# A hybrid diffusion step on one core: block 1's x loaded behind w_ada, its lora-downs moved into the recurrence list, lora-up shared out between ScalarE and GpSimd

## The chip, the core and the metric

The kernel runs on one NeuronCore of a Trainium2 chip. Its engines work side by side: TensorE (PE in the profile; PEld is its weight load), VectorE (DVE), ScalarE (ACT), GpSimd (POOL) and SyncE (SP), whose queue issues most of the transfers. Each engine runs its own instructions in the order in which they stand, and waits on semaphores where it needs another engine or a transfer. The metric is the device time of one execution in microseconds; lower is better.

## What is computed

One layer for 2176 tokens, 128 of context and 2048 of an image, each with 1024 channels. In the reference, cut to what matters here:

```python
mod = silu(c) @ w_ada + b_ada                    # shift, scale, gate of 1024 each, per kind of token
h   = rmsnorm(x, norm_g) * (1 + scale) + shift
r, k, v, g_a, b_gate, c_gate, u_conv, g_b = split(h @ w_in)     # 8 parts of 512 channels
r, k, v = token_shift(r, k, v)                   # q + mu * (0.5 * (prev + next) - q)
# _wkv, for both directions e:
lw = tanh(h @ decay_down[e])                     # 1024 -> 64     "lora-down"
w  = decay_w0[e] + lw @ decay_up[e]              # 64 -> 512      "lora-up"
la = h @ iclr_down[e]
a  = sigmoid(iclr_bias[e] + la @ iclr_up[e])
decay = exp(-exp(-softplus(-w) - 0.5))
kk = k * kk_scale, normalised per head
# then a delta-rule scan over the tokens in both directions, group norm, a gate
# group B: y = b_gate * conv3(c_gate * u_conv) * silu(g_b)
# both groups @ w_out, gate, residual; at the end one more rmsnorm
```

## The kernel before

All of it is in float32. A product on TensorE is made of three: each operand is split into a high part, rounded to the format TensorE reads, and a low part, the rest; high times high, high times low and low times high are summed. ScalarE usually makes the high part (a copy), VectorE or GpSimd the low part (a subtraction). A weight tile of `w_in` (128 rows of output, 512 KB) comes in by `raw_w` (L145), gets its high part by `high_w` (L150) and its low part by `low_w` (L154), and both parts are written back (L155), so that later thirds load them ready-made.

The program has three phases; the change lies in the opening of the first. Phase 1 goes over the tokens in blocks of 384 (`BLK`), two blocks to a third. For each third it forms the normalised `h` of both blocks, the lora-downs, then `recurrence`: eight units, four groups of 128 channels times two blocks. A unit makes the products of v, k, g and r (`mmv`, `mmk`, `mmg`, `mmr`), the lora-ups (`upa` for the learning rate, `upw` for the decay, L452), the sums per head (`psss` from kk, `psbb`), and writes the operands of the scan to HBM (`scr_ops` from the tile `xs`, L330). Then comes group B, with `mmb`, `mmc`, `mmu`, `mmgb`; inside it x of the next third is loaded and normalised (`x2`, `x3`), and the gate rows of `w_ada` come in (`wgate`).

Order: outside the recurrence a scheduler orders the instructions of each engine at build time. In the recurrence two lists of words, `UNIT_FIRST` and `UNIT`, give the order by hand for PE, DVE, ACT and POOL.

The opening before: `w_ada` comes in four slices of two pieces, 1 MB each (L265); PE forms the modulation rows from them (`psrow`, L212), VectorE copies these (`modrow`), PE turns them (`psmod`), and VectorE forms gs and sh, one pair for each half of the channels. Block 0's x (`x0`) is squared, summed by PE (`psq`), rooted on ScalarE (`rt`, L241), inverted on VectorE (L243). `make_h` then runs per 128 channels: L170 on VectorE (x times gs times rt), L171 on ScalarE (plus sh: the high part), L172 on VectorE (the low part). `first_products` forms block 0's products with the lora weights w32, w33 and with the k and r weights w4, w0 (all `mmf`) in two halves of the channels, as the halves of h appear. `lora_down` takes such a product through Tanh or Copy on ScalarE into `lf` (L664), and VectorE makes a high and a low part of each direction, `lw` (a cast, L668, a subtraction, L669). For block 1 it forms the products itself (`mml`, 48 of them). `load_up` loads the lora-up weights (`upraw`, 1 MB) and splits them into `ups` on VectorE (L125, L126).

Buffers: the pool `hl` holds two large tiles of tag "h", first the `w_ada` slices `wadas1` and `wadas2`, later h and others; tag "x" of `ta_` holds one tile, x0, then `upraw`, then `xs`, then x2; tag "upx" of `ca` holds x1, then `ups`. A new tile waits until the readers of the one before it in its buffer are done.

## Time and profile before

| | |
|---|---|
| median of 3 runs | 1640.9 us (1639.54 to 1645.43) |
| profiled execution | 1643.1 us, span 1641.3 us |
| mean granted TensorE clock | 0.967 |
| busy, share of the span | PE 92%, DVE 70%, ACT 47%, POOL 34% |
| chain that ended last | PE 66%, DVE 15%, DMA 8%, issue 5%, ACT 3% |
| the stretch of the change | 0 to 90.5 us (the opening and unit 0's products) |
| recurrence of the first third | 90.5 to 240 us, PE 144.92 us busy |
| its group B | 240 to 392 us |

A row of the timeline gives the start, the time from the first start to the last end of a run of like instructions, engine, line, operation, output and inputs, shapes, the count, and in brackets how long the engine had stood idle before and what ended that. A row of the windows gives a stretch, its length, the busy time of PE, PEld, DVE, ACT and POOL with the number of instructions, the granted clock, the share of the DMA engines and GB/s. A row of the waits gives who waited for whom, the sum, how often, and the longest. Line numbers are those of the kernel before; behind the change, lines past 256 are one to seven higher.

### The profile page before, as it was taken

The numbers are of one execution on the slowest core, as the hardware profiler recorded it, in microseconds if no ns is written. First come the engines' busy times: TensorE is split into PE (matmuls) and PEld (weight loads), VectorE is DVE, ScalarE is ACT, GpSimd is POOL, SyncE is SP. The second block draws the span as 40 slices with busy tenths as digits, with TensorE's granted clock in tenths as the row PEclk, the third lists the DMA queues.
The fourth block names the chain that finished last, engine by engine and source line by source line (L and its number), as shares of the span: only waits on it lengthen the run. The fifth ranks groups of instructions, "written<-read, shape, count | busy, mean of one in ns | idle before, by whom it ended". The sixth has DMA issues, their size and how long they took to land.

```text
span 1641.3 us, 41749 instructions
## 1 busy us (share of the span) xinstructions
PE 1518.0 (92%) x17364; PEld 1401.0 (85%) x17364; DVE 1141.3 (70%) x1960; ACT 773.5 (47%) x1494; POOL 560.8 (34%) x961
## 2 busy tenths in 40 slices
PE   5899989999999999999999989999898897599998
PEld 2899988889999999999999988888787786478786
DVE  5899993744699945459974456898888987446433
ACT  4466652511555413136531137778677776322222
POOL 0034330000233200013314507788778766112221
PEclk7799999999999999999999999999999998899999
DMA  9559998654578864438986635656566654455442
GB/s 372 199 148 263 271 258 291 239 193 162 153 209 216 225 224 165 163 115 253 243 240 231 229 104 156 176 154 184 155 183 179 162 144 151 118 170 173 136 147 96
DMA packets 204589, 313.94 MB, mean 191 GB/s; under 512 B 58088, under 2 KB 147560, under 8 KB 190320
## 3 DMA queue, kind: packets, MB, share of 16 engines
q1 hardware_dynamic: 168816, 311.13, 61.7%
q10 hardware_dynamic: 35584, 0.14, 1.5%
q8 instruction: 136, 2.23, 0.6%
q14 instruction: 53, 0.43, 0.1%
HBM read 208.05 MB, written 103.17 MB: 190 GB/s over the span
## 4 chain that ended last, share of the span: by engine, by line
PE 66%; DVE 15%; DMA 8%; issue 5%; ACT 3%; POOL 1%; SPq 1%; ACTq 0%; DVEq 0%; POOLq 0%
PE psE L1185 5%; PE psu L1500 4%; PE psS L1216 4%; PE psu L1501 3%; PE psu L1502 3%; PE psFm L1018 2%; PE psX L1167 2%; PE psGm L1018 2%; PE mmc L182 2%; PE mmb L184 2%; PE mmb L182 2%; PE mmb L183 2%; PE mmc L184 2%; PE mmc L183 2%; PE mmgb L182 1%
## 5 line engine op out<-in xcount | busy, mean ns | idle before, releaser
L1090 POOL TENSOR_TENSOR zt<-zt,ztmp 128x30 f32<-128x30 f32 (+7 forms) x510 | 206.8, 405 | 39.7
L1087 POOL TENSOR_TENSOR ztmp<-ab,zt 128x60 f32<-128x60 f32 (+7 forms) x255 | 136.5, 535 | 103.4 <-DVE ab L1078 79.7
L410 POOL TENSOR_TENSOR sh<-rawl 128x384 f32<-128x384 f32 (+1 forms) x48 | 48.0, 1017 | 252.1 <-ACT rawl L401 252.1
L1216 PE MATMUL psS<-sv,E 128*64 128x64 f32 x2176 | 101.8, 228 | 27.9 <-DVE so L1242 13.7
L1216 PEld LDWEIGHTS psS<-sv,E 128*64 128x64 f32 x2176 | 83.3, 138 | 46.1 <-issue 17.1
L1190 DVE TENSOR_TENSOR E<-psE,msk 128x512 f32<-128x512 f32 x136 | 90.9, 684 | 16.0 <-PE psE L1185 15.0
L1242 DVE TENSOR_TENSOR sv<-psS,pc 64x128 f32<-64x128 f32 x254 | 64.1, 275 | 43.5 <-PE psS L1216 42.6
L1565 POOL TENSOR_TENSOR z<-z,x 128x512 f32<-128x512 f32 x32 | 42.9, 1342 | 150.1 <-DVE z L1559 100.5
L1171 ACT ACTIVATE stf<-psX 64x512 f32<-64x512 f32 x136 | 80.5, 592 | 16.6 <-PE psX L1167 14.3
L434 POOL TENSOR_TENSOR hsl<-sq,hsh 128x384 fp32r<-128x384 f32 (+1 forms) x24 | 35.6, 1483 | 141.1 <-ACT hsh L429 141.1
L182 PE MATMUL mmg<-h,w 128*128 128x384 f32 (+1 forms) x216 | 70.8, 328 | 0.0
L183 PE MATMUL mmg<-h,w 128*128 128x384 f32 (+1 forms) x216 | 70.7, 327 | 0.0
L184 PE MATMUL mmg<-h,w 128*128 128x384 f32 (+1 forms) x216 | 70.6, 327 | 0.0
L182 PE MATMUL mmb<-h,w 128*128 128x384 f32 (+1 forms) x192 | 62.9, 328 | 5.7 <-DMA w<-scr_wsp 4.0
L182 PE MATMUL mmv<-h,w 128*128 128x384 f32 (+1 forms) x192 | 64.3, 335 | 2.8 <-ACT lf L664 2.2
L182 PE MATMUL mmc<-h,w 128*128 128x384 f32 (+1 forms) x192 | 64.1, 334 | 0.0
L184 PE MATMUL mmc<-h,w 128*128 128x384 f32 (+1 forms) x192 | 63.5, 331 | 0.6 <-DVE w L154 0.6
L184 PE MATMUL mmb<-h,w 128*128 128x384 f32 (+1 forms) x192 | 62.8, 327 | 1.2 <-DVE w L154 1.2
L183 PE MATMUL mmv<-h,w 128*128 128x384 f32 (+1 forms) x192 | 63.6, 331 | 0.0
L184 PE MATMUL mmv<-h,w 128*128 128x384 f32 (+1 forms) x192 | 63.5, 331 | 0.0
L183 PE MATMUL mmc<-h,w 128*128 128x384 f32 (+1 forms) x192 | 63.3, 330 | 0.0
L184 PE MATMUL mmu<-h,w 128*128 128x384 f32 (+1 forms) x192 | 62.6, 326 | 0.6 <-DVE w L154 0.6
(311 smaller groups left out, 5007.4 us busy)
## 6 DMA issues: line engine op xcount, KB each, us to landing
w<-scr_wsp SPq DMA_DIRECT2D x68, 1024.0 KB, 5.6
scr_wsp<-w SPq DMA_DIRECT2D x34, 1024.0 KB, 6.0
rr<-scr_ops SPq DMA_DIRECT2D x32, 1024.0 KB, 5.6
scr_ops<-xs SPq DMA_DIRECT2D x160, 192.0 KB, 6.2
wr<-in_win SPq DMA_DIRECT2D x34, 512.0 KB, 6.6
x<-in_x SPq DMA_DIRECT2D x17, 512.0 KB, 3.5
wadas<-in_wada SPq DMA_DIRECT2D x8, 1024.0 KB, 15.1
sv<-scr_vt SPq DMA_DIRECT2D x32, 256.0 KB, 3.8
```

The source lines that it names most:

```text
L182: T.matmul(ps[:, :n], w[:, 0, k], hh[:, 0, k, :n], start=k == 0, stop=False)
L183: T.matmul(ps[:, :n], w[:, 0, k], hh[:, 1, k, :n], start=False, stop=False)
L184: T.matmul(ps[:, :n], w[:, 1, k], hh[:, 0, k, :n], start=False, stop=k == 7)
L1018: T.matmul(dst(h, a, er), w[hr_, u, :], x(hr_, u), start=True, stop=True)
L1087: G.tensor_tensor(tv, ab[:, j:j + 2, j + 2:32].unsqueeze(1).broadcast_to((128, kn, 2, n)), zt[:, :kn, j:j + 2].unsqueeze(3).broadcast_to(( ...
L1090: G.tensor_tensor(zt[:, :kn, j + 2:32], zt[:, :kn, j + 2:32], tv[:, :, r], ALU.subtract)
L1171: P.activation(g.fs[64:128, :, hd, e::2], g.ps["X"][e][hr_].rearrange("p a (b t) -> p b a t", b=2), AF.Copy, scale=-1.0)
L1185: T.matmul(pe[r, i, hd, :].rearrange("p (b t) -> p b t", b=2), lt[:, b, hd, us.start + k + i], rt[:, :, hd, us.start + k + i], start=True, ...
L1190: V.tensor_tensor(g.E[n][:, k:k + 2].rearrange("p a b c -> p (a b) c"), pe[:].rearrange("p a b c -> p (a b) c"), B.msk[:, ME[g.d]].unsquee ...
L1216: T.matmul(g.sp[i // 4][r, q, hd, :], g.E[n][:, k, hd, r], g.sv[:, u, hd, :], start=True, stop=True)
L1242: V.tensor_tensor(dst, g.sp[i // 4][0:64, q], B.pc[0:64, d, 2 * p:2 * p + 2, c:c + 1].broadcast_to((64, 2, 64)), ALU.mult)
L1500: T.matmul(ps[:], mh[:, n], hi[:, cs], start=start and n == 0, stop=False)
```

## The change

Five things are done in the opening of phase 1.

1. x1 is loaded behind all of `w_ada`, between the weights w4 and w0, into the "h" buffer of `wadas1`, and no longer ahead of the last four pieces. w4 and w0 are asked for one step later in the program.
2. Block 1's norm stands behind all of block 0's first products. The lora's second half comes ahead of k and r, which run over all eight channel groups at a stretch.
3. Block 1's `lora_down` is called from the recurrence's list, at the first product on block 1, and so is the load of w12.
4. `load_up` casts on ScalarE and subtracts on GpSimd. The v weight w8 goes into the tile `wv` in tag "x", and its low part is made on GpSimd.
5. `lf` takes tag "bs" in place of "sq". In the first third `xs` takes an "h" buffer, so tag "x" is free for x2 once `wv` is read.

```diff
@@ -122,8 +122,8 @@
         parts = ca.tile([128, 8, 512], F32R, tag="upx", name="ups")
         hi, lo = [parts[:, i:i + 4].rearrange("p (n d) c -> p n d c", d=2) for i in (0, 4)]
         for n in range(2):
-            V.tensor_copy(hi[:, n], raw[:, n])
-            V.tensor_tensor(lo[:, n], raw[:, n], hi[:, n].bitcast(F32), ALU.subtract)
+            P.copy(hi[:, n], raw[:, n])
+            G.tensor_tensor(lo[:, n], raw[:, n], hi[:, n].bitcast(F32), ALU.subtract)
             for d in range(2):
                 up[n, d] = (hi[:, n, d], lo[:, n, d])
 
@@ -145,8 +145,8 @@
         nc.sync.dma_start(raw[:], A["win"][cb])
         return raw
 
-    def high_w(cb, raw):
-        w = wp.tile([128, 2, 8, 128], F32R, tag="w", name=f"w{cb}_{K.u()}", bufs=4)
+    def high_w(cb, raw, w=None):
+        w = w or wp.tile([128, 2, 8, 128], F32R, tag="w", name=f"w{cb}_{K.u()}", bufs=4)
         P.copy(w[:, 0], raw[:])
         return w
 
@@ -250,11 +250,11 @@
     hs = {}
     psf = []
 
-    def first_products(ws, ks):
+    def first_products(ws, ks, at=None):
         n = BLK[0][1]
         if ks[0] == 0:
             psf.extend(pmm.tile([128, 384], F32, tag="mm", name=f"mmf{i}_{K.u()}") for i in range(len(ws)))
-        for ps, w in zip(psf[-len(ws):], ws):
+        for ps, w in zip(psf[-len(ws):] if at is None else psf[at:], ws):
             products(ps, w, hs[0], n, ks)
 
     psm = {}
@@ -268,9 +268,10 @@
             x0 = load_x(0)
         if i == 1:
             wlora = [load_w(32), load_w(33)]
-            x1 = load_x(1, ca, "upx")
-        if i == 2:
-            ws0 = [load_w(cb) for cb in (4, 0)]
+        if i == 3:
+            ws0 = [load_w(4)]
+            x1 = load_x(1, hl, "h")
+            ws0.append(load_w(0))
         rows = tp.tile([128, 512], F32, tag="pv", name=f"modrow{b}", bufs=1)
         V.tensor_copy(rows[:], pr[:])
         hf = b % 2
@@ -292,11 +293,11 @@
         if i == 1:
             h0 = make_h(0, xb[0])
             next(h0)
-            xb[1] = norm(1, x1, V)
             first_products(wlora, range(4))
     next(h0)
-    first_products(ws0, range(4))
-    first_products(wlora + ws0, range(4, 8))
+    first_products(wlora, range(4, 8), 0)
+    first_products(ws0, range(8))
+    xb[1] = norm(1, x1, V)
 
 
     NRAW = 3
@@ -339,7 +340,7 @@
 
         one = lambda u, tag, pool=ta_, b=1, dt=F32: pool.tile([128, 384], dt, tag=tag, name=f"{tag}_{u.g}_{u.j}_{K.u()}", bufs=b)
         two = lambda u, tag: ta_.tile([128, 2, 384], F32, tag=tag, name=f"{tag}_{u.g}_{u.j}_{K.u()}", bufs=1)
-        xs = ta_.tile([128, 8, 384], F32, tag="x", name=f"xs{t3}")
+        xs = ta_.tile([128, 8, 384], F32, tag="x", name=f"xs{t3}") if t3 else hl.tile([128, 8, 384], F32, tag="h", name=f"xs{t3}")
         slot = dict(al=xs[:, 0:2], rh=xs[:, 2:4], ka=xs[:, 4:6], be=xs[:, 6:8])
         U = []
         for i, (g, j) in enumerate(units):
@@ -363,6 +364,9 @@
                 following[x] = dense(wts[x], hs[js[0]], BLK[js[0]][1], "cugb"["krvg".index(x)])
                 return
             u = U[i]
+            if u.j not in lws:
+                lws[u.j] = lora_down(u.j, *wlora, None)
+                wts["g"] = load_w(12)
             if x not in u.ps:
                 u.ps[x] = dense(wts[x], hs[u.j], u.n, x)
             if u.last:
@@ -660,7 +664,7 @@
         lw = [ta_.tile([128, 384], F32R, tag=f"lw{i}_{nm}", name=f"lw{i}_{j}") for i in range(4)]
         for which, (w, fn) in enumerate(((wd, AF.Tanh), (wi, AF.Copy))):
             ps = pre[which] if pre else dense(w, hs[j], n, f"l{which}")
-            f = ta_.tile([128, 384], F32, tag="sq", name=f"lf{which}_{j}", bufs=1)
+            f = ta_.tile([128, 384], F32, tag="bs", name=f"lf{which}_{j}", bufs=1)
             P.activation(f[:, :n], ps[:, :n], fn)
             for d in range(2):
                 a, b = slice(d * 64, d * 64 + 64), slice(64 - d * 64, 128 - d * 64)
@@ -675,14 +679,17 @@
         pre = {}
         for j in js:
             if j not in hs:
-                if t3 == 0:
-                    pre[0] = psf[2:]
-                    ws = ws0 + [load_w(cb) for cb in (8, 12)]
-                    nc.sync.dma_start(smask[:], A["cst"][:, 128:512])
                 run(make_h(j, xb[j]))
-            lws[j] = lora_down(j, wd, wi, psf[:2] if j == 0 else None)
-        if t3 == 0:
-            load_up()
+            if t3 or j == 0:
+                lws[j] = lora_down(j, wd, wi, psf[:2] if j == 0 else None)
+            if t3 == 0 and j == 0:
+                pre[0] = psf[2:]
+                nc.sync.dma_start(smask[:], A["cst"][:, 128:512])
+                load_up()
+                raw = raw_w(8)
+                wv = high_w(8, raw, ta_.tile([128, 2, 8, 128], F32R, tag="x", name="wv"))
+                low_w(8, raw, wv, G)
+                ws = ws0 + [wv, None]
         if t3:
             ws = [load_w(cb) for cb in (4, 0, 8, 12)]
         wts = dict(zip("krvg", ws))
```

On SP's queue, behind the last pieces of `w_ada` (`wadas`); `x_216` and `x_313` are x1, `wr_7` w4, `wr_9` w0, `wr_13` w8, `upraw` the lora-up weights, and `scr_wsp` the written-back parts. Before:

```order
L145 DMA wr_3_210<-in_win 128x1024 [waits DMAHW1_49]
L199 DMA x_216<-in_xt 128x8x384 [waits DMAHW2_49]
L265 DMA wadas_137<-in_wada 128x2048 [waits DMAHW3_49]
L265 DMA wadas_137<-in_wada 128x2048 [waits DMAHW4_49]
L265 DMA wadas_136<-in_wada 128x2048 [waits DMAHW5_49]
L265 DMA wadas_137<-in_wada 128x2048 [waits DMAHW6_49]
L681 DMA smask<-in_cst 128x384 [waits DMAHW7_49]
L155 DMA scr_wsp<-w_2_206 128x2048 [waits DMAHW0_49,DVE_49]
L145 DMA wr_7_326<-in_win 128x1024 [waits DMAHW1_49]
L155 DMA scr_wsp<-w_4_212 128x2048 [waits DMAHW2_49,DVE_49]
L145 DMA wr_9_332<-in_win 128x1024 [waits DMAHW3_49]
```

The same stretch in the changed kernel:

```order
L265 DMA wadas_137<-in_wada 128x2048 [waits DMAHW5_49]
L687 DMA smask<-in_cst 128x384 [waits DMAHW6_49]
L155 DMA scr_wsp<-w_2_206 128x2048 [waits DMAHW7_49,DVE_49]
L145 DMA wr_7_307<-in_win 128x1024 [waits DMAHW0_49]
L155 DMA scr_wsp<-w_4_212 128x2048 [waits DMAHW1_49,DVE_49]
L145 DMA wr_9_315<-in_win 128x1024 [waits DMAHW2_49]
L199 DMA x_313<-in_xt 128x8x384 [waits DMAHW4_49,DMAHW3_49,PE_49]
L155 DMA scr_wsp<-w_8_309 128x2048 [waits DVE_49]
L145 DMA wr_13_505<-in_win 128x1024 [waits DMAHW5_49,DMAHW0_49]
```

x1 has moved from ahead of four `w_ada` pieces to behind w0, and waits for PE, which must have read `wadas1`. Further on the same queue, in unit 0's spills, x2 (`x_2815`) now stands:

```order
L331 DMA scr_ops_59<-xs_536 128x384 [waits DMAHW4_49]
L199 DMA x_2815<-in_xt 128x8x384 [waits DMAHW5_49,PE_49]
L155 DMA scr_wsp<-w_55_820 128x2048 [waits DMAHW6_49,DVE_49]
```

Before, it stood behind the whole recurrence, in group B.

On VectorE, from the end of block 0's h; `rt_284` and `rt_460` are block 1's inverse roots, `lw_0` the lora-down parts of block 0 and `lw_1` those of block 1, `h_509` and `h_511` block 1's h. Before:

```order
L243 RECIPROCAL rt_284<-rt_284 128x128 x3
L172 SCALAR_TENSOR_TENSOR h_229<-x_149,sh_363,h_229 128x256
L154 TENSOR_TENSOR w_10_334<-wr_9_332,w_10_334 128x1024
L170 SCALAR_TENSOR_TENSOR x_216<-x_216,gs_224,rt_284 128x384 x4
L170 SCALAR_TENSOR_TENSOR x_216<-x_216,gs_362,rt_284 128x384 x4
L172 SCALAR_TENSOR_TENSOR h_509<-x_216,sh_225,h_509 128x384 x4
L668 CAST lw_0_480<-lf_0_484 64x384
L668 CAST lw_0_481<-lf_0_484 64x384
L172 SCALAR_TENSOR_TENSOR h_509<-x_216,sh_363,h_509 128x384 x4
L417 TENSOR_TENSOR sh_0_21_617<-rawc_468 128x128
L669 TENSOR_TENSOR lw_0_480<-lf_0_484,lw_0_480 64x384
L669 TENSOR_TENSOR lw_0_481<-lf_0_484,lw_0_481 64x384
```

In the changed kernel, from the end of block 0's first lora-down:

```order
L243 RECIPROCAL rt_460<-rt_460 128x128 x3
L423 SCALAR_TENSOR_TENSOR ok_0_17_549<-sh_0_16_545,dv,q_0_0_14_540 128x384
L672 CAST lw_0_482<-lf_0_490 64x384
L672 CAST lw_0_483<-lf_0_490 64x384
L170 SCALAR_TENSOR_TENSOR x_313<-x_313,gs_222,rt_460 128x384 x4
L170 SCALAR_TENSOR_TENSOR x_313<-x_313,gs_327,rt_460 128x384 x4
L673 TENSOR_TENSOR lw_0_482<-lf_0_490,lw_0_482 64x384
L673 TENSOR_TENSOR lw_0_483<-lf_0_490,lw_0_483 64x384
L172 SCALAR_TENSOR_TENSOR h_511<-x_313,sh_223,h_511 128x384 x4
L172 SCALAR_TENSOR_TENSOR h_511<-x_313,sh_328,h_511 128x384 x4
```

The reciprocal of block 1 and its eight L170 now stand behind block 0's first lora-down, and the eight stand ahead of the subtractions of the second.

On PE, from the end of the first products; `mml` are block 1's lora-downs. Before:

```order
L182 MATMUL mml_17_538<-h_509,w_2_206 128x384 [waits PE_49,Activation_49]
L182 MATMUL mml_18_569<-h_509,w_4_212 128x384 [waits Activation_49]
L183 MATMUL mml_17_538<-h_509,w_2_206 128x384 [waits DVE_49]
...
L184 MATMUL mml_18_569<-h_509,w_4_212 128x384
L452 MATMUL upa_20_614<-lw_0_482,ups 128x384 [waits DVE_49,Activation_49]
...
L182 MATMUL mmv_640<-h_229,w_14_498 128x384 [waits Activation_49]
...
L439 MATMUL psss_0_665<-hsh_0_25_627,onr 128x384 [waits Activation_49]
L440 MATMUL psss_0_665<-hsl_0_27_632,onr 128x384 [waits Pool_49]
```

The same place in the changed kernel:

```order
L227 MATMUL psq_457<-hslq_454,onf 128x384 [waits DVE_49]
L456 MATMUL upa_15_542<-lw_0_482,ups 128x384 [waits DVE_49,PE_49,Activation_49]
L456 MATMUL upa_15_542<-lw_0_482,ups 128x384 [waits Pool_49]
...
L182 MATMUL mmv_568<-h_227,wv 128x384 [waits Activation_49]
L183 MATMUL mmv_568<-h_227,wv 128x384
L184 MATMUL mmv_568<-h_227,wv 128x384 [waits Pool_49]
...
L443 MATMUL psss_0_593<-hsh_0_20_555,onr 128x384 [waits Activation_49]
L444 MATMUL psss_0_593<-hsl_0_22_560,onr 128x384 [waits Pool_49]
L182 MATMUL mml_27_603<-h_511,w_2_206 128x384 [waits Activation_49]
```

`mml` has moved from ahead of `upa` to behind `psss`, and the sum of squares `psq` of block 1 to the end of the first products; `upa` and `mmv` now also wait for GpSimd.

## The prediction

> **What bounds the kernel now.** I read the windows of the stretch that the change touches first, then the timelines of PE, DVE, ACT and POOL from 40 to 93 us, then the waits behind it. The first fence gives, per stretch, each engine's busy time, the granted clock and the share of the DMA engines.
>
> ```profile
> 35.00:40.00 5.00, 5.00 (x40) 3.28 (x36) 2.28 (x5) 1.04 (x2) 0.00 (x0) 1.00 1.03 423
> 40.00:45.00 5.00, 2.97 (x20) 1.77 (x12) 3.25 (x11) 2.81 (x6) 0.00 (x0) 0.77 0.60 248
> 69.80:90.50 20.70, 17.69 (x85) 16.84 (x85) 14.28 (x20) 9.99 (x20) 4.02 (x4) 0.84 0.42 153
> 90.50:240.00 149.50, 144.92 (x829) 141.52 (x827) 140.35 (x176) 92.70 (x165) 55.15 (x42) 1.00 0.96 252
> 300.00:340.00 40.00, 34.92 (x181) 30.07 (x180) 25.68 (x50) 12.86 (x20) 1.38 (x1) 0.96 0.66 233
> ```
>
> The DMA engines bound the first 41 us (share 1.03, 423 GB/s). From 90.5 us PE is busy 144.92 of 149.5 us: whatever makes it reach that point later is added to the end nearly one for one. So I ask when PE ends unit 0's last product (mmg), which it does at 90.4 now.
>
> ```profile
> 61.49 0.51 PE L182 MATMUL mml<-h,w 128*128 128x384 f32 x2
> 69.81 0.86 PE L452 MATMUL upa<-lw,ups 128*128 128x384 f32 x4
> 71.50 1.09 PE L452 MATMUL upw<-lw,ups 128*128 128x384 f32 x4 [0.83 <-ACT lf L664]
> 74.77 0.69 PE L182 MATMUL mmv<-h,w 128*128 128x384 f32 x1 [2.18 <-ACT lf L664]
> 81.91 0.34 PE L182 MATMUL mmk<-h,w 128*128 128x384 f32 x1
> 90.08 0.33 PE L184 MATMUL mmg<-h,w 128*128 128x384 f32 x1
> ```
>
> Between 61.49 and 69.81 PE forms block 1's 48 lora-down products (8.3 us) without a wait. They lie there under the VectorE work that upa needs:
>
> ```profile
> 48.86 2.57 DVE L243 RECIPROCAL rt<-rt 128x128 f32<-128x128 f32 x3
> 51.35 0.39 DVE L172 SCALAR_TENSOR_TENSOR h<-x,sh,h 128x256 fp32r<-128x256 f32 x1
> 52.79 4.33 DVE L170 SCALAR_TENSOR_TENSOR x<-x,gs,rt 128x384 f32<-128x384 f32 x8
> 59.14 0.74 DVE L668 CAST lw<-lf 64x384 fp32r<-64x384 f32 x2
> 62.71 1.14 DVE L669 TENSOR_TENSOR lw<-lf,lw 64x384 fp32r<-64x384 f32 x2
> 63.88 1.29 DVE L125 CAST ups<-upraw 128x1024 fp32r<-128x1024 f32 x2
> 65.09 0.61 DVE L419 SCALAR_TENSOR_TENSOR ok<-sh,dv,q 128x384 f32<-128x384 f32 x1
> 66.38 2.36 DVE L126 TENSOR_TENSOR ups<-upraw,ups 128x1024 fp32r<-128x1024 f32 x2
> 69.95 2.37 DVE L154 TENSOR_TENSOR w<-wr,w 128x1024 fp32r<-128x1024 f32 x2
> 82.11 0.56 DVE L442 TENSOR_SCALAR sq<-psss 128x384 f32<-128x384 f32 x1 [5.44 <-PE psss L440]
> ```
>
> Block 1's norm (the reciprocal at 48.86) is over before block 0's h is (51.35 + 0.39 = 51.74).
>
> **Part by part: x1 behind w_ada.** A load of x is 1536 KB, 1.57 MB; at 410 GB/s, a round figure under the 423 above, it takes 3.8 us.
>
> ```profile
> x<-in_xt SPq DMA_DIRECT2D x2, 1536.0 KB, 11.1
> 41.21 1.05 ACT L150 CAST w<-wr 128x1024 fp32r<-128x1024 f32 x1 [4.31 <-DMA wr<-in_win]
> 45.72 0.56 ACT L241 ACTIVATE rt<-psq,eps 128x384 f32<-128x384 f32 x1
> 56.53 1.28 ACT L664 ACT_TABLE_LOAD   x1 [0.89 <-PE mmf L184]
> 57.83 0.49 ACT L664 ACTIVATE lf<-mmf 128x384 f32<-128x384 f32 x1
> 60.50 0.58 ACT L405 ACTIVATE q<-mmf,dv 128x384 f32<-128x384 f32 x1
> ```
>
> With it out of the way, w4 lands at about 41.2 - 3.8 = 37.4, w0 at 41 and x1 itself at about 45. The end of block 0's h moves less than the loads, since the last w_ada products and gs still stand ahead of it and w4's low part (L154) no longer does: from 51.7 to about 50.5. That is the change's gain.
>
> **The norm behind the first products, and the price of it.** PE's products of lora on block 0 end 1 to 5 us after the last L172 (three late products, or 24 of the slow 0.32 us). With the table load and the Tanh (1.28 + 0.49) the first lf is done between 53.9 and 57.2; I take L = 56.4, near the upper end, since these products stand interleaved with k's and r's. From L the rows above lead to upa, which reads the lora-down parts of block 0: the cast of ssq and the copies of k (about 1.5, q alone 0.58), a table load back to Sqrt (1.28) and rt (0.56), L + 3.3; the reciprocal, 2.5, L + 5.8; ok and two casts, 1.3, L + 7.1; eight L170 of x1, 4.3, L + 11.4, which stand ahead of the last two subtractions of lora (1.1). So upa starts at L + 12.5 = 68.9, 0.9 earlier than its 69.81, but the 48 products of block 1 are now behind it. Before, PE needs 20.6 us from 69.81 to the end of mmg, of which 3.0 were waits for lf (0.83 + 2.18). After: 20.6 - 3.0 + 8.3 = 25.9, so mmg ends at 68.9 + 25.9 = 94.8: **+4.4 us**. By the bounds of L, upa starts between 66.4 and 69.7: +1.9 to +5.2. To break even it would have to start at 90.4 - 25.9 = 64.5.
>
> The two switches of table that are new beside this chain are priced by the 1.28 us row, and the next ACTIVATE starts 0.02 us behind it (57.83). The Trainium skill ("ScalarE: Activation LUTs", What ACT_TABLE_LOAD costs) gives 1283 ns for the load and another 1380 ns for a drain; this trace shows the first and not the second, and the one switch in the chain would cost 1.4 us more by the page.
>
> **Lora-up split off VectorE.** VectorE loses 1.29 + 2.36 of ups and 1.2 of w8. They don't come off the chain, which is the reciprocal, L170 and lora now. GpSimd gets three subtractions, and what these do to VectorE is the second price:
>
> ```profile
> 95.33 1.40 POOL L434 TENSOR_TENSOR hsl<-sq,hsh 128x384 fp32r<-128x384 f32 x1 [6.03 <-ACT hsh L429]
> 95.77 1.37 DVE L498 TENSOR_TENSOR bs<-kd 128x384 f32<-128x384 f32 x1
> 156.57 0.55 DVE L498 TENSOR_TENSOR bs<-kd 128x384 f32<-128x384 f32 x1
> 104.61 2.55 DVE L444 RECIPROCAL sq<-sq 128x384 f32<-128x384 f32 x1
> 105.25 2.41 POOL L154 TENSOR_TENSOR w<-wr,w 128x1024 fp32r<-128x1024 f32 x1 [1.95 <-ACT w L150]
> 114.49 1.22 DVE L154 TENSOR_TENSOR w<-wr,w 128x1024 fp32r<-128x1024 f32 x1
> ```
>
> L498 takes 0.55 us, but 1.37 when a GpSimd subtraction began 0.44 us ahead of it: it ends 0.41 us behind that. The reciprocal is not slowed (2.55) by a 2.41 us subtraction beneath it. So instructions with two operands from SBUF take turns with GpSimd. In the changed order ACT casts ups behind rt and the second lf, so GpSimd subtracts from about L + 4.9 to L + 9.7: the first half of that lies under the reciprocal up to L + 5.8, the rest (some 3.9) stands against ok and L170. The third, wv, starts about with the last L170 and stands against lora's subtractions (up to 2.4). Bounds 0 and +6.3; nearest the L498 row would be the upper end, but the last of them may fall between instructions: I take **+4.5 us**.
>
> The Trainium skill ("SBUF — State Buffer", SBUF: two separate sides) has GpSimd and VectorE share a port pair as "an exclusive lock, not a bandwidth split", held for a whole instruction, against VectorE's instructions with two SBUF inputs. The L498 and reciprocal rows agree with it, and by it alone the sum would hold 6.3 here.
>
> **Behind upa.** mmv needs wv's low part only now, at about 71; GpSimd is done with it then. Unit 0's chain on VectorE (L442 and the reciprocal) stood right behind psss, level with mmk (82.11 and 81.91). Now the casts and subtractions of block 1's second lora product (0.74 + 1.14) and w12's low part (1.2) stand between the last mml and it, so it starts some 3 us behind mmk. Does PE feel that? In the stretch behind, these were its longest waits:
>
> ```profile
> PE mmk L184 <- DVE w L154: 2.7, 3, 1.4
> ```
>
> VectorE is what PE waits for there, but it has 149.5 - 140.35 = 9.2 us of idle to catch up with: 0 to +3, I take **+1**.
>
> **x2 early.** Its load moves from group B, behind the recurrence, into unit 0's spills on SP's queue.
>
> ```profile
> 253.85 0.45 SPq L199 DMA_DIRECT2D x<-in_xt  x1
> 98.04 2.19 SPq L330 DMA_DIRECT2D scr_ops<-xs  x4
> 100.15 0.34 PE L184 MATMUL mmv<-h,w 128*128 128x384 f32 x1
> ACT ssq L234 <- DMA x<-in_xt: 4.9, 2, 3.2
> PE psgr L212 <- DMA wgate<-in_wada: 6.7, 1, 6.7
> ```
>
> SP issues those spills from 98.04 to 100.2. The load waits there for PE's mmv of the second unit, which ends at 100.5, so SP's queue, on which all spills and weights behind it stand, is held by little. But its 3.8 us of transfer enter a stretch whose DMA share is 0.96: 0 to +3.8, and I take **+0.5**, since a unit's weights are asked for one unit ahead. In group B, ACT no longer waits for x2 (part of 4.9 us), while the scheduler puts block 2's norm later there and block 3's too. The stretch 300 to 340 holds 5.1 us of PE idle, so -5.1 to +4: I take **-1**.
>
> Sum: 4.4 + 4.5 + 1 + 0.5 - 1 = **+9.4** on the profiled execution's 1643.1 us (span 1641.3): 1652.5. That execution is 2.2 above the median of the runs, 1640.9; against the median the forecast is **1650.3 us**. What a measurement here can tell from no change is about 0.5%, 8.2 us: below 1632.7 it is faster, above 1649.1 slower.
>
> **Rivals.** (1) *No turn-taking on the path*: GpSimd's subtractions fall under the reciprocal and into VectorE's waits for lf and rt, as the one at 105.25 does under a reciprocal. Against it stands the place: ups is cast only behind rt. Without the 4.5: 1645.8. (2) *The transfers bite*: x2's load pushes weights and spills of a saturated stretch by its 3.8 us in full, and the later norm in group B costs PE 1 us where I took a gain of 1. For it speaks the 0.96, against it that PE's longest waits there are for VectorE and none for a transfer. With 3.8 in place of 0.5, and +1 in place of -1, 1650.3 + 5.3 = 1655.6. (3) *Not slower*: with x2 in SBUF 150 us early, its norm never holds group B, and the 5.1 us of PE idle between 300 and 340 go whole. It decides once the opening loses under 5.1, that is with upa's start at the early bound and no turn-taking: 1640.9 + 1.9 - 5.1 = 1637.7. Against it: the longest PE wait there is for wgate (6.7), not for x2. (4) *The change doesn't do what it says*: x1's wait on PE's reading of w_ada (its buffer) might hold SP, behind which w8, w12 and ups stand. The last w_ada product is over before x1's bytes could flow (about 41), so I fold it into the first term.
>
> **How the numbers follow.** Forecast 0.44, own range 1647.5 to 1653.5; (1) 0.27; (2) 0.16; (3) 0.13. To hold 8 in 10 I cut the lower half of (1) and the most of (3), and let (2) stand in full: 1643 to 1657. Faster needs (3) at its far end, with the wgate wait gone too: 0.05. Slower: two thirds of the forecast's case (0.29) and (2), 0.45. No change: 0.50.
>
> **What would show it.** In the changed kernel's timeline: L172 of block 0 ends at about 50.5 (right: the load's gain is real); PE idle of some 10 us between psq and upa; upa's start at 68.9 plus the turn-taking, 73 (under 65 the forecast is wrong from the start); L170 or L673 rows of VectorE stretched to 1.5 us and more beside POOL's L126 rows (if they keep their 0.54 each, rival 1); mml behind psss, mmg's end at about 99 to 100; the window of 150 us behind it as busy as before (under 143 of 149.5: rival 2); PE idle of 5 us in the 40 us from about 309 (gone: rival 3).

## The result, and the profile after

The changed kernel takes 1654.0 us (median of 4 runs, 1652.1 to 1657.5) against 1640.2 for the kernel before; the ratio is 1.008, with a 95% interval of 1.0052 to 1.0109. A second comparison on another chip (the last run below, 12 executions) gave 1649.5 against 1639.8 and 1.006 (1.0037 to 1.0084). It is slower by 0.6 to 0.8%, 10 to 14 us; the forecast was 1650.3.

The profiled execution of the changed kernel took 1657.5 us (span 1655.7), 3.5 above its median. First PE around unit 0, in the timeline (lines from 257 on are numbered one to seven higher than before):

```profile
56.97 0.44 PE L227 MATMUL psq<-hslq,onf 128*128 128x384 f32 x1 [0.52 <-DVE hslq L219]
70.79 0.98 PE L456 MATMUL upa<-lw,ups 128*128 128x384 f32 x2 [13.38 <-DVE lw L673]
73.49 1.01 PE L456 MATMUL upa<-lw,ups 128*128 128x384 f32 x2 [1.72 <-DVE lw L673]
81.12 0.33 PE L182 MATMUL mml<-h,w 128*128 128x384 f32 x1
89.29 0.33 PE L184 MATMUL mml<-h,w 128*128 128x384 f32 x1
97.64 0.34 PE L184 MATMUL mmg<-h,w 128*128 128x384 f32 x1
```

PE stands idle for 13.38 us ahead of upa, where it formed block 1's lora-down products before, and forms them from 81.1 to 89.6 instead. The last product of unit 0 ends at 98.0; before it ended at 90.4. What PE waited for lay on VectorE, whose timeline shows the chain and what lay beside it on GpSimd and ScalarE:

```profile
49.83 0.74 DVE L172 SCALAR_TENSOR_TENSOR h<-x,sh,h 128x128 fp32r<-128x128 f32 x2
55.06 0.49 ACT L668 ACTIVATE lf<-mmf 128x384 f32<-128x384 f32 x1
58.79 2.58 DVE L243 RECIPROCAL rt<-rt 128x128 f32<-128x128 f32 x3
60.15 4.96 POOL L126 TENSOR_TENSOR ups<-upraw,ups 128x1024 fp32r<-128x1024 f32 x2 [2.76 <-ACT ups L125]
61.28 1.63 DVE L423 SCALAR_TENSOR_TENSOR ok<-sh,dv,q 128x384 f32<-128x384 f32 x1
62.84 2.88 DVE L672 CAST lw<-lf 64x384 fp32r<-64x384 f32 x2
65.75 4.32 DVE L170 SCALAR_TENSOR_TENSOR x<-x,gs,rt 128x384 f32<-128x384 f32 x8
70.10 3.34 DVE L673 TENSOR_TENSOR lw<-lf,lw 64x384 fp32r<-64x384 f32 x2
70.67 2.35 POOL L154 TENSOR_TENSOR wv<-wr,wv 128x1024 fp32r<-128x1024 f32 x1 [5.56 <-ACT wv L150]
```

Against the rows of the kernel before (0.61, 0.74 and 1.14 for ok, two casts and two subtractions), these took 1.0, 2.1 and 2.2 us longer, beside the GpSimd subtractions: 5.4 us together, 3.2 of them ahead of the first half of upa and 2.2 ahead of the second. The eight L170, between the two bursts, kept their 0.54 each.

Behind unit 0, the windows:

```profile
98.00:252.00 154.00, 145.94 (x829) 141.53 (x828) 146.03 (x180) 93.17 (x166) 52.74 (x42) 1.00 0.96 258
252.00:426.00 174.00, 163.54 (x888) 150.72 (x889) 89.84 (x176) 48.89 (x79) 7.05 (x6) 0.96 0.61 210
```

The recurrence needs 154.0 us for about the products that took 149.5 (829 matmuls in each); group B is shorter than before. The loss grew and shrank again, then. A table over all runs is made from the same marks of PE's timelines: the end of unit 0's last product, the start of psss in the second and the eighth unit and in the first unit of the second third, and the first product of phase 2 (psX, the end of phase 1). The first row is in us, all others are the difference to it. Each profile is one execution, all columns but the last two come from it; the ratios are against the kernel before on the same chip. The kernel before has one profile only, and most of the others were taken on other chips, where its median lay between 1639.8 and 1648.0 us.

| | unit 0's end | second unit | eighth unit | second third | end of phase 1 | ratio | 95% |
|---|---|---|---|---|---|---|---|
| before (us) | 90.4 | 100.3 | 220.4 | 422.6 | 986.7 | 1 | |
| changed | +7.6 | +8.0 | +12.0 | +7.9 | +8.0 | 1.008 | 1.0052 to 1.0109 |
| changed, again | +6.4 | +6.9 | +12.7 | +5.2 | +3.5 | 1.006 | 1.0037 to 1.0084 |
| a_low_v | +8.4 | +8.8 | +14.4 | +10.2 | +8.8 | 1.0065 | 1.0038 to 1.0091 |
| a_ups_v | +4.2 | +4.7 | +9.8 | +2.9 | +2.8 | 1.0024 | 1.0000 to 1.0049 |
| a_lora_ahead | +8.0 | +8.0 | +10.8 | +4.5 | +5.1 | 1.0061 | 1.0037 to 1.0085 |
| a_x1_early | +6.6 | +7.0 | +9.6 | +6.6 | +7.5 | 1.0068 | 1.0038 to 1.0097 |
| a_both_back | +2.3 | +2.2 | +5.4 | -2.0 | -3.6 | 1.0001 | 0.9975 to 1.0027 |
| a_x2_late | +6.6 | +7.0 | +8.0 | +2.5 | +6.7 | 1.0031 | 1.0011 to 1.0052 |
| b_x1_late | +11.9 | +11.9 | +11.9 | +10.4 | +9.7 | 1.0083 | 1.0058 to 1.0109 |
| b_split | -0.3 | -0.3 | -0.6 | +0.7 | +3.6 | 0.9978 | 0.9956 to 1.0000 |
| b_x2_early | -0.3 | -0.3 | +0.2 | -4.3 | -0.5 | 0.9983 | 0.9960 to 1.0006 |
| b_cast | -3.6 | -3.6 | -4.1 | -8.6 | -10.1 | 0.9982 | 0.9958 to 1.0007 |
| b_x2_cast | -3.6 | -3.6 | -3.5 | -8.2 | -4.0 | 0.9950 | 0.9927 to 0.9972 |

Names with a_ are the changed kernel with something undone, names with b_ the kernel before with one thing added. The first two marks differ by 1.1 to 1.2 us between the two executions of the changed kernel; the marks behind group B scatter by 3 to 5 us, and the totals by more. So the opening is judged by its marks, the whole by the ratio.

### The profile page after: what moved, and what is told of

Read it like the earlier page. It is cut to its first block, busy times and chain, and to the rows that moved or that the text cites. A ratio compares the mean times of both kernels' runs of the same rounds, so it can differ in the third digit from the quotient of the medians.

```text
span 1655.7 us, 41734 instructions
## 1 busy us (share of the span) xinstructions
PE 1523.4 (92%) x17364; PEld 1406.7 (85%) x17364; DVE 1147.0 (69%) x1955; ACT 777.2 (47%) x1498; POOL 559.7 (34%) x964
## 4 chain that ended last, share of the span: by engine, by line
PE 69%; DVE 13%; DMA 8%; issue 5%; ACT 3%; ACTq 1%; SPq 0%; DVEq 0%; POOL 0%
PE psE L1192 6%; PE psS L1223 4%; PE psu L1507 4%; PE psu L1508 3%; PE psu L1509 3%; PE psFm L1025 2%; PE mmb L182 2%; PE mmb L184 2%; PE mmb L183 2%; PE psX L1174 2%; PE mmc L182 2%; DMA scr_ops<-xs 2%; PE mmc L184 2%; PE mmc L183 2%; PE psGm L1025 2%
## 5 line engine op out<-in xcount | busy, mean ns | idle before, releaser
L1178 ACT ACTIVATE stf<-psX 64x512 f32<-64x512 f32 x136 | 80.3, 590 | 16.8 <-PE psX L1174 14.4
L184 PE MATMUL mmg<-h,w 128*128 128x384 f32 (+1 forms) x216 | 70.8, 328 | 1.8 <-POOL w L154 1.8
L182 PE MATMUL mmg<-h,w 128*128 128x384 f32 (+1 forms) x216 | 70.8, 328 | 0.0
L182 PE MATMUL mmb<-h,w 128*128 128x384 f32 (+1 forms) x192 | 63.6, 331 | 5.7 <-DMA w<-scr_wsp 4.0
L219 POOL TENSOR_TENSOR hslq<-ssq,hshq 128x384 fp32r<-128x384 f32 (+1 forms) x4 | 4.7, 1175 | 175.2 <-ACT hshq L218 175.2
L184 PE MATMUL mmk<-h,w 128*128 128x384 f32 (+1 forms) x184 | 60.4, 328 | 3.8 <-DVE w L154 3.8
L184 PE MATMUL mmb<-h,w 128*128 128x384 f32 (+1 forms) x192 | 63.5, 331 | 0.0
L183 PE MATMUL mmb<-h,w 128*128 128x384 f32 (+1 forms) x192 | 63.2, 329 | 0.0
```

Of the source, the lines that this page charges most:

```text
L182: T.matmul(ps[:, :n], w[:, 0, k], hh[:, 0, k, :n], start=k == 0, stop=False)
L183: T.matmul(ps[:, :n], w[:, 0, k], hh[:, 1, k, :n], start=False, stop=False)
L184: T.matmul(ps[:, :n], w[:, 1, k], hh[:, 0, k, :n], start=False, stop=k == 7)
L1178: P.activation(g.fs[64:128, :, hd, e::2], g.ps["X"][e][hr_].rearrange("p a (b t) -> p b a t", b=2), AF.Copy, scale=-1.0)
```

## The experiments

The first theory was that block 1's late norm and GpSimd's turns with VectorE are the loss. Its rivals blame the place in the list, or the split as such, or VectorE's load. A turn, here and below, is the time that a VectorE instruction takes longer while a subtraction of GpSimd runs beside it.

### The place of the 48 products, and the place of the norm

**a_lora_ahead**, the list's part undone in the changed kernel:

```diff
-            if u.j not in lws:
-                lws[u.j] = lora_down(u.j, *wlora, None)
-                wts["g"] = load_w(12)
...
-            if t3 or j == 0:
-                lws[j] = lora_down(j, wd, wi, psf[:2] if j == 0 else None)
+            lws[j] = lora_down(j, wd, wi, psf[:2] if j == 0 else None)
...
-                ws = ws0 + [wv, None]
+                ws = ws0 + [wv, load_w(12)]
```

> The changed kernel, but block 1's lora-downs (and the load of w12) stand ahead of the recurrence's list again, as before the change; x1 and its norm stay late. Theory 1 (the late norm is the cause, the list only puts the 48 products where h of block 1 exists): the products start when h appears, about 74, and end about 83, then upw, mmv, mmk and mmg take 13.5, so the last product ends at 96 to 98, as in the changed kernel (98.0) or little earlier; 1651 to 1655. Rival (the place in the list is the cause): unit 0 is back near its 90.4, the kernel at 1645 to 1648.

Unit 0's last product ended at 98.4 against 98.0, just above the range of the first theory: nothing is gained. The products wait for h of block 1, as PE's timeline shows, and this is made no sooner:

```profile
67.50 1.01 PE L182 MATMUL mml<-h,w 128*128 128x384 f32 x2 [9.64 <-ACT h L171]
```

**a_x1_early**, x1 and its norm put back:

```diff
         if i == 1:
             wlora = [load_w(32), load_w(33)]
+            x1 = load_x(1, ca, "upx")
         if i == 3:
             ws0 = [load_w(4)]
-            x1 = load_x(1, hl, "h")
             ws0.append(load_w(0))
...
             next(h0)
+            xb[1] = norm(1, x1, V)
             first_products(wlora, range(4))
...
     first_products(ws0, range(8))
-    xb[1] = norm(1, x1, V)
```

> The changed kernel, but x1 is loaded ahead of the last w_ada pieces and its norm stands where it did before the change; the list, the split of lora-up and the early x2 stay. Theory 1 (late norm and GpSimd's subtractions): the reciprocal and L170 are off the way to upa, which starts between 66 and 70; unit 0's last product ends 25.9 later, at 92 to 96, and the kernel takes 1643 to 1648. Rival (the list and the split alone make the loss, the place of the norm does not matter): 97 to 99 and 1653 to 1655.

The first theory was not met: the last product ended at 97.0, 1.0 us earlier than in the changed kernel, above its range and at the lower end of the rival's. The total, 1650.7 (a ratio of 1.0068), lies between the two forecasts. Its timeline (rows of POOL, DVE and PE, in order of time) shows why the norm's absence brings so little:

```profile
63.72 4.95 POOL L126 TENSOR_TENSOR ups<-upraw,ups 128x1024 fp32r<-128x1024 f32 x2 [3.36 <-ACT ups L125]
63.77 2.71 DVE L423 SCALAR_TENSOR_TENSOR ok<-sh,dv,q 128x384 f32<-128x384 f32 x1
66.40 2.88 DVE L672 CAST lw<-lf 64x384 fp32r<-64x384 f32 x2
69.31 3.29 DVE L673 TENSOR_TENSOR lw<-lf,lw 64x384 fp32r<-64x384 f32 x2
70.01 0.98 PE L456 MATMUL upa<-lw,ups 128*128 128x384 f32 x2 [8.38 <-DVE lw L673]
```

PE is idle again, for 8.38 us: h of block 1 is made early now, ahead of lora's parts on VectorE, and GpSimd's turns come on top. The 48 products could have been formed in this gap, but they stand behind psss in the list.

**b_x1_late**, the kernel before with x1 and the norm late (the edit of the change's first two parts, nothing else):

> The kernel before with only x1 moved behind all of w_ada and its norm behind the first products (and these in the changed order); lora-downs ahead of the list, lora-up on VectorE. Theory 1 (late norm): block 1's h appears some 10 us later than before, its 48 products start near 70 and end near 77 to 79, unit 0's last product ends 17.6 later, at 95 to 97, and the kernel takes 1645 to 1649. Rival (the split and the list are the cause): the last product ends within 2 us of 90.4 and the kernel takes 1639 to 1643.

The loss was larger than expected, 11.9 us at unit 0's end, 1.0083 in total. PE's timeline:

```profile
66.18 1.01 PE L182 MATMUL mml<-h,w 128*128 128x384 f32 x2 [9.86 <-ACT h L171]
72.81 0.69 PE L183 MATMUL mml<-h,w 128*128 128x384 f32 x1 [5.62 <-DVE h L172]
82.89 0.86 PE L453 MATMUL upa<-lw,ups 128*128 128x384 f32 x4
```

PE waits 9.9 and 5.6 us for h of block 1 and then forms the 48 products with upa queued behind them. The changed kernel, which adds the list and the split to this, is 4.3 us better at that mark. So the late norm alone is enough for a loss, yet taking it out of the changed kernel gave back only 1.0. This gave another theory, called theory 2 in the next expectation: the 48 products have to lie under VectorE's work ahead of upa, and either edit alone takes that cover away.

**a_both_back**, both undone together:

> The changed kernel with x1 and its norm early again and block 1's lora-downs ahead of the list again; the split, wv and the early x2 stay. Theory 2 (the 48 products must lie under VectorE's work ahead of upa; either edit alone takes that cover away, so undoing one gives back 1 us or nothing, as seen, and undoing both gives all): they run from 61.5 to 70 again, upa starts at 70 to 72.5 with GpSimd's turns, unit 0's last product ends at 89.5 to 92.5, total 4 to 10 us under the changed kernel. Rival (the two losses are separate ones): 6.6 less 0.4 gives 95 to 97, total as the runs with one of them undone.

The last product ended at 92.7, 0.2 above the expected range, and the ratio to the kernel before is 1.0001. The two losses are one. With neither edit unit 0 ends 2.3 us behind the kernel before, with the list alone 6.6, with the late norm alone 8.0, with both 7.6 (6.4 in the second execution): either edit alone costs 4.3 to 5.7 us, and the other adds next to nothing. So undoing the one gave 1.0, the other -0.4, both 5.3 us (4.1 against the second execution, on the same chip). What is left, 2.3 us, shows in the timeline as a longer wait ahead of mmv (3.08 us, 2.18 before) and a later upa:

```profile
71.04 1.18 PE L453 MATMUL upa<-lw,ups 128*128 128x384 f32 x4 [1.20 <-DVE lw L670]
73.07 2.52 POOL L154 TENSOR_TENSOR wv<-wr,wv 128x1024 fp32r<-128x1024 f32 x1 [3.37 <-ACT wv L150]
73.42 3.18 DVE L670 TENSOR_TENSOR lw<-lf,lw 64x384 fp32r<-64x384 f32 x2
77.23 0.69 PE L182 MATMUL mmv<-h,wv 128*128 128x384 f32 x1 [3.08 <-ACT lf L665]
```

The subtractions of block 1's lora parts stretch to 3.18 beside GpSimd's wv, and lf, for which mmv waits, comes behind them.

### GpSimd's turns with VectorE

**a_low_v**, all three subtractions of the changed kernel back on VectorE:

```diff
-            G.tensor_tensor(lo[:, n], raw[:, n], hi[:, n].bitcast(F32), ALU.subtract)
+            V.tensor_tensor(lo[:, n], raw[:, n], hi[:, n].bitcast(F32), ALU.subtract)
...
-                low_w(8, raw, wv, G)
+                low_w(8, raw, wv, V)
```

> The changed kernel, but the three subtractions that it gave to GpSimd (two of ups, one of wv) are made by VectorE again; the casts stay on ScalarE. Theory 1 (GpSimd's subtractions hold VectorE up ahead of upa): in the changed kernel ok took 1.63 us, the two casts of lw 2.88 and the two subtractions of lw 3.34 beside them. Those go back to about 0.61, 0.74 and 1.14, which takes off 5.3; VectorE gets 2.36 of ups ahead of upa, so unit 0's last product ends about 3 us earlier, near 95, and the kernel takes about 1651. Rival (VectorE is simply overloaded, and the relief was worth its price): 3.6 us more work on VectorE, the kernel at 1655 to 1658.

The turns are gone (ok 0.52, the casts 0.73), and upa started at 68.1, 2.7 earlier. But unit 0's end was 98.8, so the expectation missed: wv's subtraction now stands behind h of block 1 on VectorE, and PE waits for it in the middle of mmv:

```profile
76.06 0.44 PE L184 MATMUL mmv<-h,wv 128*128 128x384 f32 x1 [2.83 <-DVE wv L154]
```

The total, 1650.5, is near the 1651 expected, but its ratio lies among those of the changed kernel, so it shows no gain. **a_ups_v** leaves wv on GpSimd and has only the first of the two edits above:

> The changed kernel with the two subtractions of ups on VectorE and that of wv left on GpSimd. Theory 1 (turn-taking ahead of upa): ok and the casts of lw take 0.6 and 0.74, upa starts near 68 as in the run with all three on VectorE (68.1), and since wv is not made behind h of block 1 any more, mmv does not wait 2.8 us for it; unit 0's last product ends at 95 to 96.5, 1.5 to 3 us before the changed kernel's 98.0. Rival (no gain, as with all three: what VectorE gains by the turns it pays in work): 98 to 99.

Its timeline, rows of DVE, PE and POOL:

```profile
61.12 0.52 DVE L423 SCALAR_TENSOR_TENSOR ok<-sh,dv,q 128x384 f32<-128x384 f32 x1
61.56 0.73 DVE L672 CAST lw<-lf 64x384 fp32r<-64x384 f32 x2
68.51 0.66 PE L456 MATMUL upa<-lw,ups 128*128 128x384 f32 x1 [11.26 <-ACT h L171]
70.24 7.27 DVE L172 SCALAR_TENSOR_TENSOR h<-x,sh,h 128x384 fp32r<-128x384 f32 x8
70.78 2.38 POOL L154 TENSOR_TENSOR wv<-wr,wv 128x1024 fp32r<-128x1024 f32 x1 [13.56 <-ACT wv L150]
```

Unit 0 ended at 94.7, 2.2 to 3.3 us before the two executions of the changed kernel; the ratio fell to 1.0024 (1.006 for the changed kernel on the same chip, with intervals that just overlap). wv's subtraction costs VectorE 2.2 us here too (eight L172 take 7.27, where the changed kernel has 5.07), but behind upa, where PE doesn't wait for it. So turns cost only what lies on the path: GpSimd starts wv at the same moment as in the changed kernel (70.78 against 70.67), but there the last subtraction of lw stood beside it, and here that is over.

**b_split** gives only the split to the kernel before:

```diff
-            V.tensor_copy(hi[:, n], raw[:, n])
-            V.tensor_tensor(lo[:, n], raw[:, n], hi[:, n].bitcast(F32), ALU.subtract)
+            P.copy(hi[:, n], raw[:, n])
+            G.tensor_tensor(lo[:, n], raw[:, n], hi[:, n].bitcast(F32), ALU.subtract)
```

> The kernel before with only the lora-up split: casts of ups on ScalarE, subtractions on GpSimd; x1, its norm and the lora-downs as before. Theory 1 (the split costs by GpSimd's turns with VectorE and gains by 3.65 us less work there, both under the 48 products): the two L126 run beside ok and lora's casts and subtractions, which stretch by 2 to 4 us, upa starts within 1.5 us of 69.8, unit 0's last product ends between 89.5 and 92, total 1638 to 1643. Rival (the split alone costs what the change costs): last product at 94 or later, 1645 or more.

As expected: ok takes 2.65 and the casts 2.94 beside GpSimd, upa starts 1.5 later at 71.3, and unit 0 ends at 90.1. The later upa is made up behind it: the wait ahead of mmv is 1.04 us in place of 2.18, and mmv's products take 5.8 us (75.43 to psss at 81.27) in place of 6.8. VectorE's 3.65 us less of work and the turns about cancel.

**b_cast** moves only the casts, the first and third of these lines, and leaves the subtractions on VectorE:

> The kernel before with the casts of ups on ScalarE and nothing else. Theory (VectorE 1.29 us ahead, PE's wait ahead of mmv under 1.1 us, and the 24 products of mmv at full clock): upa at 69.6, mmv 4.3 us instead of 6.8, unit 0's last product at 86.5 to 87.5, and the second third 3 to 4 us earlier; total 2 to 5 us under the kernel before. Rival (the 3.3 us seen with x2 early as well came from x2's load): last product at 89.5 to 90.5, total equal.

The timeline of PE:

```profile
69.62 0.86 PE L452 MATMUL upa<-lw,ups 128*128 128x384 f32 x4
73.16 0.45 PE L182 MATMUL mmv<-h,w 128*128 128x384 f32 x1 [1.05 <-ACT lf L664]
77.45 0.34 PE L439 MATMUL psss<-hsh,onr 128*128 128x384 f32 x1
86.45 0.33 PE L184 MATMUL mmg<-h,w 128*128 128x384 f32 x1
```

Unit 0 ends at 86.8, 3.6 us before the kernel before, though only 1.29 us of work was taken off VectorE; the last section says where the rest comes from. The total is not told from no change (0.9982, up to 1.0007).

### x2's early load

**a_x2_late** holds x2's load back in the changed kernel:

```diff
+        if t3 == 0:
+            hold = ta_.tile([128, 8, 384], F32, tag="x", name="hold")
+            one_ = wts["r"][:, 0, 0, 0:1].bitcast(F32)
+            G.tensor_tensor(hold[:, 0, 0:1], one_, one_, ALU.add)
         early = gate_rows() if t3 == 0 else first_states() if t3 == 1 else iter(())
```

> The changed kernel, with x2's load held back as before the change: a placeholder tile stands in its buffer, written by GpSimd (one 128x1 addition) once the r weight of group B is there, so x2 is loaded in group B again. Theory 1 (x2's early transfer costs in the recurrence and repays in group B): the lead over the kernel before at unit 0's last product (+7.6) stays within 1 us of that up to the eighth unit, where the changed kernel had grown to +12.0, and group B gives back 2 at the most where the changed kernel gave back 4.1; at the second third +8 to +10, in total 1652 to 1655, no gain. Rival (the growth in the recurrence is VectorE's lag behind block 1's lora parts): it grows to +12 all the same, and the second third starts at +10 to +12.

From the second to the eighth unit it fell behind the kernel before by another 1.0 us (1.4 from unit 0's end), the changed kernel by another 4.0 and 5.8 in its two executions. The rows of the changed kernel name the reason:

```profile
109.47 0.41 SPq L199 DMA_DIRECT2D x<-in_xt  x1
120.82 1.05 ACT L150 CAST w<-wr 128x1024 fp32r<-128x1024 f32 x1 [3.56 <-DMA wr<-in_win]
134.02 1.05 ACT L150 CAST w<-wr 128x1024 fp32r<-128x1024 f32 x1 [4.77 <-DMA wr<-in_win]
137.56 0.44 PE L184 MATMUL mmg<-h,w 128*128 128x384 f32 x1 [1.79 <-POOL w L154]
```

Behind x2's load the next weights come late: ScalarE waits 3.56 and 4.77 us for them, GpSimd's low part follows, and PE waits for it. With x2 late, the same two casts wait for no transfer:

```profile
116.19 1.09 ACT L150 CAST w<-wr 128x1024 fp32r<-128x1024 f32 x1
129.04 1.04 ACT L150 CAST w<-wr 128x1024 fp32r<-128x1024 f32 x1
```

Whether x2's bytes or its place on SP's queue holds the weights up was not tested. The price also hangs on what else is late: in a_lora_ahead, a_x1_early and a_both_back, with x2 as early, the growth was 2.6 to 3.2 us. The second half of the expectation missed: group B gave back 5.5 us with x2 late, more than the 4.1 of the changed kernel. The ratio, 1.0031, is below those of the changed kernel, but it was taken on another chip, and the profile's end of phase 1 (+6.7) shows no such gain.

**b_x2_early** gives the kernel before only the other buffer for xs:

```diff
-        xs = ta_.tile([128, 8, 384], F32, tag="x", name=f"xs{t3}")
+        xs = ta_.tile([128, 8, 384], F32, tag="x", name=f"xs{t3}") if t3 else hl.tile([128, 8, 384], F32, tag="h", name=f"xs{t3}")
```

> The kernel before with only the buffer of xs moved (first third in tag h), so that x2 is loaded as soon as ups is split, near 69 us, when the DMA engines are half idle. Theory 1: the recurrence is not touched (within 1 us of before at the eighth unit), and group B loses its stalls on block 2's norm: the second third starts 2 to 6 us earlier, total 1635 to 1639. Rival (the recovery seen in group B came from the later arrival there and not from x2): the second third starts within 1 us of before, total 1640.

Here x2 is loaded at 68.6, since no wv stands ahead of it in the buffer, when the DMA engines have room (their share from 68 to 73 us is 0.22 in the kernel before and 0.62 here), and the recurrence pays nothing (+0.2 at the eighth unit). Group B gave back 4.5. But b_cast, with x2 loaded at 247, gave back 4.5 too (from -4.1 to -8.6), so what shortens group B isn't shown: it took 173 to 177 us from its first mmb to the second third in the changed kernel, in all runs with xs in tag h and in b_cast, 179 to 181 in the three others. The waits that differ are those of PE for wgate (none to 8.3 us) and for the copies of its rows. That stays open. The total is not told from no change.

**b_x2_cast** has both, b_x2_early's line and b_cast's:

> As the run with xs moved and x2 early, and ups cast on ScalarE, its subtraction staying on VectorE. Theory 1 (VectorE's work ahead of upa and mmv is what PE waits for, 0.83 + 2.18 us in the kernel before): VectorE is 1.29 us ahead, mmv starts 0.5 to 1.3 us earlier and unit 0's last product ends at 89.1 to 90; total 0 to 1.5 us under the run with x2 alone. Rival (PE's 48 products end at 69.8 and nothing behind them is VectorE's): no difference.

Unit 0 ended 3.3 us before that of b_x2_early, more than the 0.1 to 1 expected, and the ratio to the kernel before is 0.9950 (0.9927 to 0.9972). This is the one version that is faster than the kernel before beyond its interval, by 0.5%: lora-downs and norm as before the change, xs in tag h, and of the split only the casts. On its chip these are some 8 us; the profile shows 3.5 of them at the eighth unit and 4.0 at the end of phase 1, and where the rest lies is not shown.

### The same kernel again

**after_again** is the changed kernel without an edit:

> The changed kernel once more, beside the others on one chip. If the 6 us by which its profiled execution fell behind in phase 2, whose instructions did not change, were a property of the kernel, its phase 2 takes 462 to 463 us again and the total stands 13 to 15 over the kernel before; if they came from the clock of that execution, phase 2 takes between 455 and 460 and the total stands 8 to 12 over.

The window of phase 2 in the first execution, and then in the second:

```profile
994.70:1457.20 462.50, 401.45 (x10400) 361.13 (x10397) 361.65 (x718) 321.87 (x627) 311.97 (x690) 0.94 0.59 160
```

```profile
990.10:1448.50 458.40, 396.35 (x10401) 356.07 (x10397) 361.42 (x718) 322.26 (x627) 313.87 (x690) 0.95 0.58 162
```

In the first, phase 2 took 5.5 us longer than in the kernel before (457.0), at a granted clock of 0.94 against 0.95; in the second 1.4 longer, and the total stood 9.7 over. Over the 14 profiles, phase 2, which no edit touches, took 452.8 to 462.8; between the two kernels some transfers change order on SP's queue there. So the 6 us beyond phase 1 in the first profile are not a loss that the change makes in every execution; with one profile for each kernel, no more can be said of them.

## Why the prediction was right, and where its steps were not

The direction and the mechanism of the opening held, and 1654.0 lies within the stated 1643 to 1657, just above the forecast's own 1647.5 to 1653.5. That the size came so near (+9.4 forecast, +13.8 and +9.7 measured) is in part luck: the terms behind the opening were off in both directions, by the end of phase 1 the two profiles were only 8.0 and 3.5 us behind, and the rest of the total lies beyond it, where nothing was forecast. The prediction had also given a higher chance to a difference within 0.5% (0.50) than to a greater loss (0.45), which is what came. By its own steps:

- **The gain of x1's place**: the last L172 of block 0 was to end at 50.5 and ends at 50.57. Right.
- **L and the chain to upa**: the first lf was to be done at 56.4, and was at 55.55, inside the bounds. Reciprocal, ok, casts, L170, subtractions came in that order; upa at 68.9 without and 73 with the turns, measured 70.8 for its first half and 73.5 for its second. That the second fits so well is chance: lf came 0.9 early and the turns were 0.9 dearer.
- **The 48 products behind psss**: the step "20.6 - 3.0 + 8.3 = 25.9" from upa to the end of mmg measured 27.2 (70.79 to 97.98), of which 1.72 is the wait between the halves of upa. It came so near because two things it left out cancelled: the 20.6 held mmv at the 6.8 us of a low granted clock (5.2 in the changed kernel), while the lora-ups took 1.1 us more than before. The end of unit 0, forecast at 99 to 100, was 98.0, and the idle of "some 10 us" was 13.4.
- **Turn-taking**: +4.5 forecast of 0 to 6.3, 5.4 in the rows, and right in kind. Its rows were partly others: the two casts of lw, with one operand from SBUF, stretched most (2.88 for 0.74), which "instructions with two operands from SBUF" did not cover, and L170 not at all. Taking the turns of ups away and paying 2.36 us of work for them brought 2.2 to 3.3 at unit 0's end (a_ups_v). Rival 1, no turns on the path, fell.
- **VectorE's lag behind upa**: +1 taken. The growth of 1.0 between the second and eighth unit with x2 late fits it, on one profile; that it comes from this lag is not shown.
- **x2 early**: +0.5 taken of 0 to 3.8. This term was mis-sized: it costs about 3 to 5 us (growth of 4.0 and 5.8 against 1.0 with x2 late). Failed was the reason given with it, that a unit's weights are asked for one unit ahead and so have time; the rows show ScalarE waiting 3.6 and 4.8 us for them. By the prediction's own mark for rival 2, under 143 us of PE in the 149.5 behind unit 0, the transfers did bite: 141.75 from 98.0 to 247.5, against 143.84 in the same stretch behind unit 0 with x2 late.
- **Group B**: -1 taken of -5.1 to +4; it gave back 4.1 and 7.5 in the two executions. Mis-sized to the other side, which hid the step before. Rival 3's mechanism was there in part (PE idle in the 40 us fell from 5.1 to 2.6), on a loss too large for it; and its cause is open, since x2 late and b_cast gave as much back.
- **Beyond phase 1** nothing was forecast, and the 6 us of the first profile were not seen again.

The prediction took the late norm and the list as one chain; the runs show what it had not said, that undoing either one alone leaves nearly the whole loss.

## What to carry to other kernels

Work that fills one engine while another prepares its next input is worth up to its length there (of 8.3 us of products, 4.3 to 5.7 were lost with the cover); before moving it or its input, ask what else could stand in the gap, and undo such edits together when testing. In this kernel GpSimd's subtractions held up VectorE's instructions beside them by up to their own length (5.4 us beside 7.3); the time to the mark was lost only where PE waited for these. So hand over what falls behind the path, or hand it to ScalarE. A buffer that lets a load start early also picks the moment: the same load was free at 69 us in the kernel before and cost about 3 to 5 us at 109 in the changed one.

## What the runs showed of the hardware that was not expected

Casts on VectorE (64x384, f32 in, one operand) took turns with GpSimd's subtraction like two-operand instructions: 2.88, 2.88 and 2.94 us for two in three kernels, 0.73 without. The Trainium skill ("SBUF — State Buffer", SBUF: two separate sides) names VectorE's two-port modes beside two SBUF inputs as what shares the pair with GpSimd; these rows agree with that, though no run shows in which mode the casts ran.

Short waits of PE were dearer than themselves, through the granted clock. In the kernel before, PE waited 0.83 and 2.18 us between 70 and 75 us, and in the window behind that the clock was 0.55 (the first fence). In b_cast it waited 0.66 and 1.05 us, and the clock stays at 1.00 (the second):

```profile
73.60:81.00 7.40, 6.23 (x21) 6.23 (x22) 2.35 (x5) 2.58 (x5) 1.01 (x1) 0.55 0.95 337
```

```profile
70.00:77.50 7.50, 5.79 (x32) 5.12 (x30) 5.38 (x10) 3.71 (x8) 0.57 (x1) 1.00 0.81 283
```

The 24 products of mmv took 6.8 us in the first (74.77 to psss at 81.56) and 4.3 in the second (73.16 to 77.45). Of the 3.6 us that the casts brought, 2.5 came so, through the clock; 1.6 came ahead of mmv, from the shorter waits and the earlier upa, and 0.5 were lost again behind it.

It is not the length of one wait that decides. In b_split none was above 1.11 us, and the one ahead of mmv was as short as in b_cast, but the clock fell all the same:

```profile
75.43 0.44 PE L182 MATMUL mmv<-h,w 128*128 128x384 f32 x1 [1.04 <-ACT lf L664]
```

```profile
73.60:81.00 7.40, 6.19 (x25) 5.87 (x26) 4.08 (x8) 2.69 (x6) 1.01 (x1) 0.77 0.98 349
```

Its three waits sum to 2.95 us (1.11, 0.80 and 1.04) between 70 and 75.5, those of the kernel before to 3.01, those of b_cast to 1.71. The sum fits these three profiles, and so it does b_x2_early (3.03, and 0.51 from 73 to 77 us) and b_x2_cast (1.73, and 1.00 there); that it is the rule is not shown.
